# Six gate projections of the merge written behind the convolution's, four kept beside the loads of the first output projection

## The chip, the cores and the metric

The kernel runs on one core of a Trainium2 chip. The metric is the device time of one execution in microseconds (us), as the median of several. The core has five engines with their own instruction rows: TensorE (PE; matmuls, and its weight loads, PEld), VectorE (DVE), ScalarE (ACT), GpSimd (POOL) and SyncE (SP), whose row here only issues DMA transfers. Engines wait for one another by semaphores, and each works off its row in order.

## The reference

One layer of a streaming encoder over 1152 tokens (a prompt of 1024 and eight groups of 16), with a width of 1024. All projections of h share one weight matrix. Branch A is a delta-rule recurrence, branch B a gated short convolution; two gates merge them.

```
h = rmsnorm(x, g_norm)
proj = h @ w_in          # [r k v w a z_a | B C xb z_b | g_a g_b]
...
y, S = wkv7_scan(wkv0, r_h, w_h, kh_h, a_h, v_h, kt_h)
...
out_a = o_a @ w_o_a
gb, gc, xb, z_b = jnp.split(pb, 4, axis=-1)
u = gc * xb
u_pad = jnp.concatenate([conv0, u], axis=1)
cv = sum(conv_w[j] * u_pad[:, j:j + T] for j in range(CONV_W))
out_b = (gb * cv * jax.nn.silu(z_b)) @ w_o_b
g_a, g_b = jnp.split(jax.nn.sigmoid(pg), 2, axis=-1)
x = x + (g_a * out_a + g_b * out_b) @ w_out
x = x + jax.nn.sigmoid(rmsnorm(x, g_ple) @ w_ple_gate) * (p @ w_ple)
```

## The kernel before

Widths of 1024 are eight tiles of 128 partitions, and the 1152 tokens lie along the free axis, in blocks of 512, 512 and 128 (`BLOCKS`, in the order 0, 1024, 512) or three of 384 (`BL3`). A projection tile ("dense") multiplies the eight tiles of h by eight 128x128 weight blocks in a split of two float16 parts: for each block of tokens three matmuls for each of the eight, so 24. `load_w` (L143 to L149) fetches one tile's weights to a stage buffer `wst...` (two of them, SP), makes the high part `whi...` on ACT and the low part `wlo...` on DVE.

The recurrence is cut into 24 steps: eight pairs of heads (7 is the last) by three blocks of tokens (step 7_2 is pair 7, block at 512), 144 chunks of 64 tokens in all. Each chunk is a chain of small matmuls with ACT and DVE work between them (tiles u, vu, sbd, c, xs; the state's copy yst on ACT). What stands ahead of the chain are the prep projections of a step (k, r, v, z), and beside all of it the convolution: `conv(j)` for eight tiles, four projections each (C, x, z_b, B), whose results go to `ob_d` in DRAM. A step's output goes through a normalisation, is turned by a PE transposition (tile py out of yc, L96), gated, and stored to `oa_d` in DRAM.

PE's order of all this is written by hand in `go()`. Seven streams, `chain` to `conv`, are generators; each step of `go()` takes the first stream that is ready by a modelled PE clock, and if none is, a piece of a projection ("fill") from prep or conv:

```
S_chain, S_tail, S_val, S_inv, S_scores, S_prep, S_conv = every = [
    Stream(k) for k in (chain, tail, values, inverse, scores, prep, conv)]
...
fills = more or [x for x in live if x.next == DENSE]
...
pe[0] = min(x.when() for x in live)
```

All other engines, and PE behind `go()`, are ordered by the tile scheduler. It may place PE instructions of the later code between those of the written order where they are free to go.

Behind `go()` comes the merge. `gate(ms[j], T_GB + j)` projects the gate g_b of tile j, with tanh, into the tile ms_j (PE tiles dgb0 to dgb7; weights whigb, wlogb), and `load_o(ob_d, j)` (L919, split at L899 and L901) fetches one tile of branch B's result in three transfers of 384 columns (stage tiles ostb, three buffers) and splits each into ohb (ACT) and olb (DVE). Eight pairs of these stand one behind the other:

```
for j in range(KT):
    gate(ms[j], T_GB + j, f"b{j}")
    obs.append(load_o(ob_d, j, f"b{j}"))
```

Then w_ob is applied: for each j, weights wstb are loaded and split, and three blocks of 24 matmuls (tiles ob) are added up over all eight tiles of obs; DVE (L948) multiplies each with the gate into ms. After it the same for branch A: gates g_a of tiles 0 and 1 (dga), eight loads of `oa_d`, then for each j a block of w_oa (tiles oa), and gate j + 2 behind it. Then w_out (oc), the per-layer embedding and the final norm.

Of the kernel before, what the change touches and what calls it, by code (L numbers as in the profile page):

```python
# [9 lines left out]
F32 = mybir.dt.float32  # L10
# [3 lines left out]
AF = mybir.ActivationFunctionType  # L14
# [6 lines left out]
NTOK = 1152  # L21
BLOCKS = [(0, 512), (1024, 128), (512, 512)]
# [4 lines left out]
IWS = 1.0 / WS  # L27
# [3 lines left out]
T_R, T_K, T_V, T_L, T_ZA, T_B, T_C, T_XB, T_ZB, T_GA, T_GB = 0, 8, 16, 24, 25, 33, 41, 49, 57, 65, 73  # L31
# [35 lines left out]
def build(nc, tc, I, O):  # L67
    with ExitStack() as top:
        _build(nc, tc, I, O, top)


def _build(nc, tc, I, O, top):
    V, A, G, PE, SP = nc.vector, nc.scalar, nc.gpsimd, nc.tensor, nc.sync
# [16 lines left out]
    def mm(out, lhsT, rhs, start, stop):  # L90
        spent(lhsT, rhs, lhsT.dtype == F32)
        PE.matmul(out, lhsT, rhs, start=start, stop=stop)  # L92
# [6 lines left out]
    dram = top.enter_context(tc.tile_pool(name="dram", bufs=1, space=bass.MemoryType.DRAM))  # L99
# [26 lines left out]
    for n, src in enumerate(("w0", "i0", "krep")):  # L126
        o, w = PN[src]
# [14 lines left out]
    def load_w(src, nm):  # L142
        wpool, WR = wcur  # L143
        st = wpool.tile([128, KT, 128], F32, tag="wst", name="wst" + nm, bufs=2)
        SP.dma_start(st, src)
        hi = wpool.tile([128, KT, 128], F16, tag="whi", name="whi" + nm, bufs=WR)
        lo = wpool.tile([128, KT, 128], F16, tag="wlo", name="wlo" + nm, bufs=WR)
        A.activation(hi, st, AF.Copy, scale=WS)  # L148
        V.scalar_tensor_tensor(out=lo, in0=st, scalar=WS, in1=hi, op0=ALU.mult, op1=ALU.subtract)  # L149
        return hi, lo  # L150
# [6 lines left out]
    def hT(k, blk, lo):  # L157
        o, n = blk
        v = hx[:, k, o:o + n].bitcast(F16)
        return v[:, n:2 * n] if lo else v[:, 0:n]  # L160

    def dense_parts(w, blk, nm):

        n = blk[1]
        hi, lo = w
        for k in range(KT):
            yield DENSE if k == 0 else MORE
            if k == 0:
                ps = psd.tile([128, 512], F32, tag="d", name="d" + nm)
            mm(ps[:, :n], hi[:, k, :], hT(k, blk, 0), start=(k == 0), stop=False)  # L170
            mm(ps[:, :n], hi[:, k, :], hT(k, blk, 1), start=False, stop=False)
            mm(ps[:, :n], lo[:, k, :], hT(k, blk, 0), start=False, stop=(k == KT - 1))
        return ps[:, :n]

    def dense(w, blk, nm):
        g = dense_parts(w, blk, nm)
        while True:
            try:
                next(g)
            except StopIteration as e:  # L180
                return e.value
# [4 lines left out]
    for nm_, names, t in (("cpk", CPK, F32), ("cph", CPH, F16)):  # L186
        w = sum(w for _, w in names)
# [17 lines left out]

    oa_d = dram.tile([8, 128, NTOK], F32, tag="oa_d", name="oa_d")
    ob_d = dram.tile([8, 128, NTOK], F32, tag="ob_d", name="ob_d")

    rk = ExitStack()
    wk = rk.enter_context(tc.tile_pool(name="wkv", bufs=2))  # L210
    cvp = rk.enter_context(tc.tile_pool(name="cvp", bufs=1))
# [532 lines left out]
    def conv(j):  # L744
# [43 lines left out]
                                   op0=ALU.mult, op1=ALU.mult)  # L788
        SP.dma_start(ob_d[j], zs)

    pairs = {}
    chunks = [0]
    steps = []
    for j in range(8):
        for g in range(3):
            f = St()
# [22 lines left out]
    class Stream:  # L819
        def __init__(self, kind):  # L820
            self.kind, self.at, self.gen, self.next, self.ready, self.cost = kind, 0, None, None, 0.0, 0.0
            self.till, self.banks = None, 0
            self.total = 8 if kind is conv else len(steps)

        def step(self):
            t = pe[0]
# [21 lines left out]
        def fill(self):  # L848
            return self.next in (DENSE, MORE)

    S_chain, S_tail, S_val, S_inv, S_scores, S_prep, S_conv = every = [
        Stream(k) for k in (chain, tail, values, inverse, scores, prep, conv)]
    may = {S_chain: lambda i: S_inv.at > i and S_val.at > i and S_tail.at >= i - 1,
           S_tail: lambda i: S_chain.at > i,
           S_val: lambda i: S_scores.at > i and S_chain.at >= i - 1 and (i < 2 or steps[i - 2].y_done),
           S_inv: lambda i: S_scores.at > i,
           S_scores: lambda i: S_prep.at > i and (i < 3 or steps[i - 3].y_done),
           S_prep: lambda i: S_chain.at >= i - 3,
           S_conv: lambda i: True}
    CONV_US, LEAD = 8 * 46.4, 4.0  # L860

    def go():
        while True:
            for x in every:
                if x.gen is None and x.at < x.total and may[x](x.at):
                    x.gen = x.kind(x.at if x is S_conv else steps[x.at])
                    x.step()
            live = [x for x in every if x.gen is not None and x.open()]
            if not live:
                return  # L870
            ready = [x for x in live if not x.fill() and x.when() <= pe[0]]
            if ready:
                ready[0].step()
                continue
            more = [x for x in live if x.next == MORE]
            fills = more or [x for x in live if x.next == DENSE]
            if fills:
                behind = S_conv.cost / CONV_US < (chunks[0] + LEAD) / 144
                fills.sort(key=lambda x: (x is S_conv) != behind)
                fills[0].step()  # L880
                continue
            pe[0] = min(x.when() for x in live)

    with tc.manual_schedule(engines={mybir.EngineType.PE}):
        go()
# [10 lines left out]
    ms = [mr.tile([128, NTOK], F32, tag=f"ms{j}", name=f"ms{j}") for j in range(KT)]  # L896

    def split_r(dst_hi, dst_lo, src, scale=1.0):
        A.activation(dst_hi, src, AF.Copy, scale=scale)  # L899
        if scale == 1.0:  # L900
            V.tensor_tensor(out=dst_lo, in0=src, in1=dst_hi.bitcast(F32), op=ALU.subtract)  # L901
        else:
            V.scalar_tensor_tensor(out=dst_lo, in0=src, scalar=scale, in1=dst_hi.bitcast(F32),
                                   op0=ALU.mult, op1=ALU.subtract)

    def load_wr(src, nm, scale=1.0):
        st = ow.tile([128, KT, 128], F32, tag="wst", name="wst" + nm, bufs=2)
        SP.dma_start(st, src)
        wh = op.tile([128, KT, 128], F32R, tag="woh", name="woh" + nm, bufs=2)
        wl_ = op.tile([128, KT, 128], F32R, tag="wol", name="wol" + nm, bufs=2)  # L910
        split_r(wh, wl_, st, scale)
        return wh, wl_

    def load_o(src, k, nm):
        h_ = oo.tile([128, NTOK], F32R, tag=f"oh{k}", name=f"oh{nm}")
        l_ = oo.tile([128, NTOK], F32R, tag=f"ol{k}", name=f"ol{nm}")
        for o, n in BL3:
            st = op.tile([128, 384], F32, tag="ost", name=f"ost{nm}_{o}", bufs=3)
            SP.dma_start(st[:, :n], src[k, :, o:o + n])  # L919
            split_r(h_[:, o:o + n], l_[:, o:o + n], st[:, :n])  # L920
        return h_, l_

    def dense_r(w, src, blk, nm):
        o, n = blk
        wh, wl_ = w
        ps = psp.tile([128, 512], F32, tag="p", name=nm)[:, :n]
        for k in range(KT):
            h_, l_ = src[k]
            mm(ps, wh[:, k, :], h_[:, o:o + n], start=(k == 0), stop=False)
            mm(ps, wh[:, k, :], l_[:, o:o + n], start=False, stop=False)  # L930
            mm(ps, wl_[:, k, :], h_[:, o:o + n], start=False, stop=(k == KT - 1))
        return ps

    def gate(dst, t, nm):
        w = load_w(I["w_in"][t], "g" + nm)
        for o, n in BLOCKS:
            A.activation(dst[:, o:o + n], dense(w, (o, n), f"g{nm}_{o}"), AF.Tanh, scale=0.5 * IWS)

    obs = []
    for j in range(KT):  # L940
        gate(ms[j], T_GB + j, f"b{j}")
        obs.append(load_o(ob_d, j, f"b{j}"))
    for j in range(KT):
        w = load_wr(I["w_ob"][j], f"b{j}")
        for blk in BL3:
            o, n = blk
            ps = dense_r(w, obs, blk, f"ob{j}_{o}")
            V.scalar_tensor_tensor(out=ms[j][:, o:o + n], in0=ms[j][:, o:o + n], scalar=1.0, in1=ps,  # L948
                                   op0=ALU.add, op1=ALU.mult)
    oas = []  # L950
    gts = {}

    def gate_a(j):
        gts[j] = op.tile([128, NTOK], F32, tag="gt", name=f"gt{j}", bufs=2)
        gate(gts[j], T_GA + j, f"a{j}")

    gate_a(0)
    gate_a(1)
    for k in range(KT):
        oas.append(load_o(oa_d, k, f"a{k}"))  # L960
    for j in range(KT):
        w = load_wr(I["w_oa"][j], f"a{j}")
        g = gts[j]
        for blk in BL3:
            o, n = blk
            ps = dense_r(w, oas, blk, f"oa{j}_{o}")
# [28 lines left out]
    xn0 = pgx[:, 2 * KT * D:].rearrange("p (k a t) -> p k a t", a=2, k=KT)  # L995
    gps = small.tile([128, 8], F32, tag="gps", name="gps", bufs=1)
    go, _ = PN["gp"]
    V.tensor_scalar(out=gps, in0=par[:, go:go + 8], scalar1=WS, scalar2=None, op0=ALU.mult)
    xrs, wos = {}, {}
# [186 lines left out]
```

## Time and profile before

| | |
|---|---|
| runs shown | 1945.39, 1945.68 and 3071.51 us, median 1945.68 |
| profiled execution | 1941.51 us, span 1939.7 us |
| busy share of the span | PE 94%, PEld 64%, DVE 65%, ACT 42%, POOL 11% |
| mean clock granted to PE | 0.988 of full speed |
| moved by DMA | 103.57 MB, 53 GB/s on average |

The span is the time between the first and the last instruction of the profiled execution; 1.8 us of it lie outside. The busy share is an average over stages: chunk chain and projections (to about 1195 us), the end of the chain (to about 1335 us), and the merge behind it. Matmuls overlap, so the duration of one is longer than its distance to the next; in PE's rows the starts are compared.

### The profile page before, as it was taken

The numbers are of one execution on the slowest core, as the hardware profiler recorded it, in microseconds if no ns is written. First come the engines' busy times: TensorE is split into PE (matmuls) and PEld (weight loads), VectorE is DVE, ScalarE is ACT, GpSimd is POOL, SyncE is SP. The second block draws the span as 40 slices with busy tenths as digits, with TensorE's granted clock in tenths as the row PEclk, the third lists the DMA queues.
The fourth block names the chain that finished last, engine by engine and source line by source line (L and its number), as shares of the span: only waits on it lengthen the run. The fifth ranks groups of instructions, "written<-read, shape, count | busy, mean of one in ns | idle before, by whom it ended". The sixth has DMA issues, their size and how long they took to land. (4 is left out here: it accounts for less than half of the span.)

```text
span 1939.7 us, 37843 instructions
## 1 busy us (share of the span) xinstructions
PE 1814.9 (94%) x15374; PEld 1248.6 (64%) x15374; DVE 1255.6 (65%) x3225; ACT 811.8 (42%) x1877; POOL 219.1 (11%) x333
## 2 busy tenths in 40 slices
PE   4999999999999999999999998799999999999997
PEld 2565665565566566566556566455698777899766
DVE  7466878787787787787877777774223311444665
ACT  6344545545446446446446445343202211332321
POOL 1010211111111111111111111110000111200000
PEclk9999999999999999999999999899999999999999
DMA  6002011101101101101101100013313311142012
GB/s 217 22 23 76 22 48 42 34 30 60 39 30 50 50 30 50 50 30 37 60 29 37 41 18 15 32 46 94 99 44 96 99 44 33 56 144 87 9 35 78
DMA packets 43758, 103.57 MB, mean 53 GB/s; under 512 B 6208, under 2 KB 21440, under 8 KB 43584
## 3 DMA queue, kind: packets, MB, share of 16 engines
q1 hardware_dynamic: 43584, 101.17, 16.3%
q8 instruction: 120, 1.97, 0.4%
q14 instruction: 54, 0.44, 0.1%
HBM read 84.40 MB, written 16.74 MB: 52 GB/s over the span
## 5 line engine op out<-in xcount | busy, mean ns | idle before, releaser
L92 PEld LDWEIGHTS <-whip 128*128 128x128 f16 x1536 | 132.3, 99 | 72.2 <-issue 3.5
L653 POOL TENSOR_SCALAR Spt<-sbd,pt 128x128 f32<-128x128 f32 x128 | 86.7, 677 | 664.8 <-DVE sbd L669 642.5
L92 PEld LDWEIGHTS <-wlop 128*128 128x128 f16 x768 | 75.4, 98 | 61.1 <-issue 1.1
L669 DVE SCALAR_TENSOR_TENSOR sbd<-u,pt,Spt 64x64 f32<-64x64 f32 x256 | 72.1, 282 | 65.3 <-PE u L92 61.6
L595 ACT ACTIVATE bdgt<-ig 64x512 f16<-64x512 f32 (+1 forms) x208 | 106.5, 512 | 2.5
L659 ACT ACTIVATE yst<-c 64x128 f32<-64x128 f32 x144 | 38.8, 270 | 151.0 <-DVE xs L658 149.7
L92 PE MATMUL dx<-hx,whiX 128*128 128x512 f16 (+1 forms) x384 | 88.4, 326 | 4.7 <-ACT sho L229 4.7
L92 PE MATMUL dgb<-hx,whigb 128*128 128x512 f16 (+1 forms) x384 | 90.5, 331 | 2.2 <-ACT whigb L148 1.6
L92 PE MATMUL dv<-hx,whip 128*128 128x512 f16 (+1 forms) x384 | 90.7, 331 | 0.0
L92 PE MATMUL dzb<-hx,whiZ 128*128 128x512 f16 (+1 forms) x384 | 88.6, 326 | 2.2 <-ACT sho L229 1.8
L92 PE MATMUL dz<-hx,whip 128*128 128x512 f16 (+1 forms) x384 | 89.5, 326 | 0.0
L92 PE MATMUL dC<-hx,whiC 128*128 128x512 f16 (+1 forms) x384 | 88.4, 327 | 1.1 <-ACT cs L750 0.6
L92 PE MATMUL dB<-hx,whiB 128*128 128x512 f16 (+1 forms) x384 | 89.1, 326 | 0.0
L92 PE MATMUL pg<-xn,pg 128*128 128x384 f16 (+1 forms) x576 | 88.9, 309 | 0.0
L92 PE MATMUL dr<-hx,whip 128*128 128x512 f16 (+1 forms) x384 | 88.9, 326 | 0.0
L92 PE MATMUL dk<-hx,whip 128*128 128x512 f16 (+1 forms) x384 | 88.1, 326 | 0.0
L92 PE MATMUL dga<-hx,whiga 128*128 128x512 f16 (+1 forms) x384 | 86.9, 326 | 0.0
L92 PEld LDWEIGHTS <-pg 128*128 128x128 f16 x768 | 66.3, 99 | 27.1 <-issue 2.4
L664 ACT ACTIVATE vu<-u 64x64 f32<-64x64 f32 x288 | 62.3, 216 | 46.8 <-PE u L92 44.1
L589 ACT ACTIVATE gt<-ig 128x512 f16<-128x512 f32 (+1 forms) x104 | 54.3, 522 | 66.0 <-PE ig L92 65.1
L596 DVE CAST_PREDICATED tt<-cph,i 128x512 f16<-128x512 uint16 (+1 forms) x104 | 61.7, 593 | 25.4 <-PE i L92 24.3
L92 PEld LDWEIGHTS u<-xs,tm 128*128 128x128 f32 x288 | 49.7, 192 | 43.9 <-DVE xs L658 28.8
(325 smaller groups left out, 4924.8 us busy)
## 6 DMA issues: line engine op xcount, KB each, us to landing
wstp<-i_w_in SPq DMA_DIRECT2D x32, 512.0 KB, 3.6
xt<-i_x SPq DMA_DIRECT2D x9, 512.0 KB, 5.5
ob_d<-zb SPq DMA_DIRECT2D x8, 576.0 KB, 2.8
ostb<-ob_d SPq DMA_DIRECT2D x24, 192.0 KB, 3.1
osta<-oa_d SPq DMA_DIRECT2D x24, 192.0 KB, 2.9
xr<-i_xT SPq DMA_DIRECT2D x8, 576.0 KB, 3.6
wstC<-i_w_in SPq DMA_DIRECT2D x8, 512.0 KB, 3.5
wstX<-i_w_in SPq DMA_DIRECT2D x8, 512.0 KB, 3.5
```

Of the source, the lines that this page charges most:

```text
L92: PE.matmul(out, lhsT, rhs, start=start, stop=stop)
L589: A.activation(Gt, pg, AF.Copy, scale=-1.0)
L595: A.activation(Gb[R, :, R], pg[R], AF.Copy, scale=-1.0)
L596: V.copy_predicated(out=Tt, mask=bc(lvt[:, b, :]).bitcast(U16), data=p1)
L653: G.tensor_scalar(out=Spt, in0=S, scalar1=pt[:, c:c + 1], scalar2=None, op0=ALU.mult)
L659: A.activation(yst[Vh, p, :], pc[Vh, 0:128], AF.Copy)
L664: A.activation(vu[Uh, c, H], pu[H, H], AF.Copy, scale=-1.0)
L669: V.scalar_tensor_tensor(out=S2[H, H], in0=pu[H, 128 + h * 64:192 + h * 64], scalar=pt[H, c:c + 1], in1=Spt[H, H], op0=ALU.mult, op1=ALU.add)
```

## The change

Gates g_b of tiles 0 to 3 and g_a of tiles 6 and 7 (`EARLY`) are no longer computed in the merge. A new generator, `gates_b`, loads the weights of one of them, runs its three blocks and stores the tanh result to a new DRAM tensor `gb_d`. Its stream, `S_gate`, is the last in the list of `go()` and may run when all eight convolution tiles are through and not all steps are finished, so its projections are fills like theirs. In the merge, ms0 to ms3 and the g_a tiles gt6 and gt7 are read back from `gb_d`. The four g_b gates that are left stand two loads of `ob_d` apart.

```
+    EARLY = [T_GB, T_GB + 1, T_GB + 2, T_GB + 3, T_GA + 6, T_GA + 7]
+    gb_d = dram.tile([len(EARLY), 128, NTOK], F32, tag="gb_d", name="gb_d")
...
+    def gates_b(j):
+
+        w = load_w(I["w_in"][EARLY[j]], f"gb{j}")
+        t = cvp.tile([128, NTOK], F32, tag="cv", name=f"gb{j}", bufs=2)
+        for o, n in BLOCKS:
+            ps = yield from dense_parts(w, (o, n), f"gb{j}_{o}")
+            A.activation(t[:, o:o + n], ps, AF.Tanh, scale=0.5 * IWS)
+        SP.dma_start(gb_d[j], t)
...
-            self.total = 8 if kind is conv else len(steps)
+            self.total = {conv: 8, gates_b: 6}.get(kind, len(steps))
...
-    S_chain, S_tail, S_val, S_inv, S_scores, S_prep, S_conv = every = [
-        Stream(k) for k in (chain, tail, values, inverse, scores, prep, conv)]
+    S_chain, S_tail, S_val, S_inv, S_scores, S_prep, S_conv, S_gate = every = [
+        Stream(k) for k in (chain, tail, values, inverse, scores, prep, conv, gates_b)]
...
-           S_conv: lambda i: True}
+           S_conv: lambda i: True,
+           S_gate: lambda i: S_conv.at == 8 and S_tail.at < len(steps)}
...
-                    x.gen = x.kind(x.at if x is S_conv else steps[x.at])
+                    x.gen = x.kind(x.at if x in (S_conv, S_gate) else steps[x.at])
...
     for j in range(KT):
-        gate(ms[j], T_GB + j, f"b{j}")
-        obs.append(load_o(ob_d, j, f"b{j}"))
+        if T_GB + j not in EARLY:
+            gate(ms[j], T_GB + j, f"b{j}")
+            for k in range(2 * (j - 4), 2 * (j - 3)):
+                obs.append(load_o(ob_d, k, f"b{k}"))
     for j in range(KT):
+        if T_GB + j in EARLY:
+            SP.dma_start(ms[j], gb_d[EARLY.index(T_GB + j)])
         w = load_wr(I["w_ob"][j], f"b{j}")
...
-        gate(gts[j], T_GA + j, f"a{j}")
+        if T_GA + j in EARLY:
+            SP.dma_start(gts[j], gb_d[EARLY.index(T_GA + j)])
+        else:
+            gate(gts[j], T_GA + j, f"a{j}")
```

The order of instructions shows it at three places. The first is PE's row behind the last projection of the convolution, in pair 6's last step. Tiles ig2, i1 and i2 belong to prep of pair 7, u and c to the chain, whig and wlog are the weights of a gate. Before:

```order
L92 MATMUL ig27_0_15901<-tt7_0_15675,bdmh_126 128x64
L92 MATMUL u6_2_3_15862<-vu6_2_15072,kbt6_2_15052 128x128
L92 LDWEIGHTS bdtn_128
L92 MATMUL i127_0_15915<-gt27_0_15910,bdtn_128 128x64
L92 LDWEIGHTS bdtn_128
L92 MATMUL i127_0_15915<-gt27_0_15910,bdtn_128 128x64
...
L92 MATMUL c6_2_4_15927<-sbd0_120,ar6_2_14728 128x128
```

With the change:

```order
L92 MATMUL ig27_0_15909<-tt7_0_15676,bdmh_127 128x64
L92 LDWEIGHTS whigb0_15858
L92 MATMUL dgb0_0_15920<-hx_97,whigb0_15858 128x512
L92 LDWEIGHTS whigb0_15858
L92 MATMUL dgb0_0_15920<-hx_97,whigb0_15858 128x512
L92 LDWEIGHTS wlogb0_15859
L92 MATMUL dgb0_0_15920<-hx_97,wlogb0_15859 128x512
L92 MATMUL u6_2_3_15870<-vu6_2_15073,kbt6_2_15053 128x128
```

Three matmuls of the first early gate stand ahead of the chain's u, and the others follow between its links.

The second place is PE's row around the last transposition, py of step 7_2. The early gates and the late ones have names of the same kind; dgb5 here is a late one, g_b of tile 5. Before:

```order
L92 LDWEIGHTS wlogb3_17561
L92 MATMUL dgb3_0_17564<-hx_97,wlogb3_17561 128x512
L96 MATMUL py7_2_17229<-ident_75,yc7_2_17205 128x128 x4
L92 LDWEIGHTS whigb3_17560
L92 MATMUL dgb3_0_17564<-hx_97,whigb3_17560 128x512
```

With the change:

```order
L92 MATMUL dgb5_1024_17925<-hx_97,whigb5_17895 128x128
L96 MATMUL py7_2_17746<-ident_75,yc7_2_17722 128x128 x4
L92 LDWEIGHTS wlogb5_17896
L92 MATMUL dgb5_1024_17925<-hx_97,wlogb5_17896 128x128
L92 LDWEIGHTS whigb5_17895
L92 MATMUL dgb5_512_17951<-hx_97,whigb5_17895 128x512
```

What stands behind py begins two gates and a block and a half later in the row of gates.

The third is SP's queue at the last store to `oa_d`. Before:

```order
L691 DMA o_wkv_p<-sbd1_121 64x64 x2
L145 DMA wstgb6_17852<-i_w_in 128x1024
L732 DMA oa_d_104<-yc7_2_17205 128x512
L919 DMA ostb0_0_17350<-ob_d_105 128x384
L919 DMA ostb0_384_17354<-ob_d_105 128x384
L919 DMA ostb0_768_17358<-ob_d_105 128x384
L919 DMA ostb1_0_17448<-ob_d_105 128x384
```

With the change:

```order
L960 DMA ms3_17776<-gb_d_106 128x1152
L694 DMA o_wkv_p<-sbd1_122 64x64 x2
L921 DMA wstb0_18230<-i_w_ob 128x1024
L735 DMA oa_d_104<-yc7_2_17722 128x512
L932 DMA ostb0_0_17867<-ob_d_105 128x384
L932 DMA ostb0_384_17871<-ob_d_105 128x384
L932 DMA ostb0_768_17875<-ob_d_105 128x384
L921 DMA wstb1_18315<-i_w_ob 128x1024
L921 DMA wstb2_18400<-i_w_ob 128x1024
L932 DMA ostb1_0_17881<-ob_d_105 128x384
```

The loads of ms and of the first output weight come ahead of the store, and two more weights stand between the first and the second tile of ostb.

## Rows read from the trace of the kernel before

**Rows 1.** Stretch, its length; busy us of PE, PEld, DVE, ACT, POOL; granted clock, DMA.
```profile
75.00:1195.00 1120.00, 1064.61 (x10398) 669.02 (x10396) 870.53 (x2317) 553.83 (x1336) 160.99 (x264) 1.00 0.12 39
1195.00:1335.00 140.00, 118.93 (x1082) 72.56 (x1080) 94.88 (x269) 60.04 (x159) 18.81 (x26) 0.93 0.11 35
1335.00:1400.00 65.00, 63.23 (x390) 36.33 (x391) 20.50 (x32) 22.91 (x44) 0.00 (x0) 1.00 0.41 134
```

**Rows 2.** Timeline of PE: start, duration, operation [idle before, releaser].
```profile
1334.90 0.66 PE L96 MATMUL py<-ident,yc 128*128 128x128 f32 x4 [0.63 <-DVE yc L723]
```

**Rows 3.** Waits of PE, 1195 to 1335: us in total, times, longest.
```profile
PE py L96 <- DVE yc L723: 6.0, 3, 4.8
```

**Rows 4.** Busy time by stretches, columns as in rows 1.
```profile
1224.00:1237.00 13.00, 5.48 (x41) 3.96 (x42) 10.54 (x42) 5.38 (x20) 1.71 (x2) 0.71 0.01 2
1237.00:1255.00 18.00, 15.95 (x112) 9.24 (x110) 10.36 (x25) 4.23 (x14) 1.21 (x2) 0.92 0.05 18
1255.00:1267.00 12.00, 9.41 (x54) 5.02 (x55) 9.36 (x22) 3.97 (x7) 1.28 (x2) 0.57 0.41 140
```

**Rows 5.** Timeline of PE, pairs of projection matmuls at 1238 and 1240.
```profile
1238.27 1.06 PE L92 MATMUL dv<-hx,whip 128*128 128x512 f16 x2
...
1240.56 0.59 PE L92 MATMUL dv<-hx,whip 128*128 128x512 f16 x2
```

**Rows 6.** Timeline of PE, starts of two blocks of a gate.
```profile
1338.68 0.59 PE L92 MATMUL dgb<-hx,whigb 128*128 128x512 f16 x2
...
1343.86 0.59 PE L92 MATMUL dgb<-hx,whigb 128*128 128x512 f16 x2
...
1349.04 0.27 PE L92 MATMUL dgb<-hx,whigb 128*128 128x128 f16 x2
...
1350.38 0.59 PE L92 MATMUL dgb<-hx,whigb 128*128 128x512 f16 x2
```

**Rows 7.** Busy time by stretches, columns as in rows 1.
```profile
1300.00:1326.00 26.00, 24.46 (x155) 13.74 (x156) 10.18 (x37) 8.72 (x29) 5.18 (x7) 1.00 0.09 26
400.00:500.00 100.00, 91.57 (x891) 59.01 (x890) 79.67 (x226) 47.23 (x122) 10.96 (x23) 1.00 0.15 48
100.00:200.00 100.00, 96.69 (x903) 57.94 (x901) 70.42 (x175) 48.77 (x112) 12.58 (x19) 1.00 0.16 51
```

**Rows 8.** Costliest groups: weight loads of prep, busy us, mean ns.
```profile
L92 PEld LDWEIGHTS <-whip 128*128 128x128 f16 x1536 | 132.3, 99 | 72.2 <-issue 3.5
```

**Rows 9.** Timeline of PE, in the first block of ob, 22 matmuls apart.
```profile
1393.34 0.33 PE L92 MATMUL ob<-ohb,wolb 128*128 128x384 f32 x1
...
1397.17 0.33 PE L92 MATMUL ob<-ohb,wohb 128*128 128x384 f32 x1
```

**Rows 10.** Timeline of ACT: a gate's weights, two triples of ob_d.
```profile
1343.84 1.06 ACT L148 ACTIVATE whigb<-wstgb 128x1024 f16<-128x1024 f32 x1 [0.31 <-PE dgb L92]
...
1351.09 1.02 ACT L899 ACTIVATE ohb<-ostb 128x384 fp32r<-128x384 f32 x2 [1.25 <-DMA ostb<-ob_d]
...
1358.10 1.03 ACT L899 ACTIVATE ohb<-ostb 128x384 fp32r<-128x384 f32 x2
```

**Rows 11.** Timeline of DVE: a gate's weights, the last triple, the first result.
```profile
1371.94 1.23 DVE L149 SCALAR_TENSOR_TENSOR wlogb<-wstgb,whigb 128x1024 f16<-128x1024 f32 x1
...
1375.19 1.15 DVE L901 TENSOR_TENSOR olb<-ostb,ohb 128x384 fp32r<-128x384 f32 x2 [2.02 <-ACT ohb L899]
...
1397.37 0.56 DVE L948 SCALAR_TENSOR_TENSOR ms<-ms,ob 128x384 f32<-128x384 f32 x1 [20.14 <-PE ob L92]
```

**Rows 12.** DMA issues: operation, count, KB each, median us to landing.
```profile
ostb<-ob_d SPq DMA_DIRECT2D x24, 192.0 KB, 3.1
...
wstgb<-i_w_in SPq DMA_DIRECT2D x8, 512.0 KB, 3.6
```

**Rows 13.** Busy time of DVE and ACT on the tile yst, two stretches.
```profile
1195.00:1335.00 140.00, 2.34 (x4) 5.93 (x22) 0.93 0.11 35
480.00:800.00 320.00, 3.31 (x6) 10.28 (x38) 1.00 0.13 43
```

## The prediction

> **What bounds the kernel now.** I read the shares of the engines first, by stretches of the span [rows 1]. From 75 to 1195 us, while projections are still left for the written order to fill with, TensorE (PE) is busy for 1064.61 of 1120 us. From 1195 to 1335 us, when the last convolution projection is through and only the chunk chain is left, it is busy for 118.93 of 140 us, at a granted clock of 0.93. Behind that, through the gates and loads, it is at 63.23 of 65 us. So the kernel is bound by PE throughout, with one hole of 21.1 us between the end of the convolution and the last transposition of the chain (py of step 7_2), which starts at 1334.90 and takes 0.66 us [rows 2]. The waits of PE in the hole say that it stands for links of the chain, above all for VectorE's yc, 6.0 us in three waits with one of 4.8 [rows 3]: latency that other matmuls could cover.
>
> The clock makes the hole larger. Before 1237 us PE is at work for 5.48 of 13 us, and behind this its granted clock lies between its levels of 1.2 and 2.4 GHz, at 0.71, 0.92 and 0.57 of full speed in three stretches [rows 4]. Two matmuls of 512 columns take 1.06 us at 1238.27 and 0.59 two microseconds later [rows 5]. A clock of 0.71 over 13 us means 7.5 us at the lower level; times the busy share of 0.42, and half of that as excess, 1.6 us. The other two stretches give 18 x 0.16 x 0.89 / 2 = 1.3 and 12 x 0.86 x 0.78 / 2 = 4.0. Together 6.9 us of the 118.93 are slow clock, not work: the hole holds 112.0 us of work at full speed in 140 us.
>
> **What the change moves.** One gate is 24 matmuls for each of its blocks of 512, 512 and 128 columns: 5.18 us (1338.68 to 1343.86) twice, and 1.34 us (1349.04 to 1350.38), 11.70 us in all [rows 6]. I counted the gate matmuls in PE's row before and after the change. Ahead of the last py stand 159 of 512 columns and 72 of 128 before, which the scheduler had put there from gb0 to gb3; with the change 360 and 191 stand there: the six early gates, all of gb4 and most of gb5. The first of them stands right behind the last convolution projection and takes turns with the chain. So 201 x 0.2158 = 43.4 us and 119 x 0.056 = 6.6 us, together 50.0 us, move ahead of the last py. No matmul is added or taken away; what can be won is time in the hole, what can be lost is cover behind it.
>
> **The hole (gain R).** The stretch from 1195 us to the last py then holds 112.0 + 50.0 = 162.0 us of work. How dense will it be? The nearest row is the end of the hole, where the chain already had scheduler-placed gates beside it: 24.46 busy of 26 us, 94.1%, at a clock of 1.00 [rows 7]. At that share it takes 172.2 us, so py starts at about 1367.2. The old hole and the moved work one after the other would be 140 + 50 = 190, so R = 17.8 us. The bounds come from the loaded stage: its loosest and its densest stretch of 100 us are busy for 91.57 and 96.69 us [rows 7], which give 176.9 and 167.5 us, R from 13.1 to 22.5.
>
> Busy time of matmuls overlaps, so it may flatter. The Trainium skill (Perfetto Trace Analysis, Identifying the Most-Contended Engine) says that matmul busy time is a bad measure and that the weight loads' busy share should be used. By that row, the loaded stage shows 669.02 of 1120 us, 59.7%, and the hole 72.56 of 140, 51.8%; 320 added loads of 0.099 us [rows 8] make 104.2, at 59.7% that is 174.5 us, and R would be 15.5, the sum 2.3 us lower. The order of the two stretches is the same by both measures.
>
> **The loads of the first output projection (loss S).** Eight triples of ost loads must be split by ScalarE (ohb) and VectorE (olb) before the first block ob0_0 can end. They still begin after the last py in both kernels, since their pool takes memory that the last store of the chain (oa_d of 7_2) frees. Before, 4.72 gates lay over them, 55.3 us; now one matmul of gb5's 128 block, gb5's last block, gb6 and gb7: 28.6 us of PE work. ob0_0 itself is 24 x 0.174 = 4.2 us (22 matmuls from 1393.34 to 1397.17) [rows 9], so without a stall it would end 33.5 us after py starts (0.66 + 28.6 + 4.2). When is the last triple there? Triples follow each other on ScalarE at 3.5 us when nothing else holds them up: two of them from 1351.09 to 1358.10 [rows 10]. By the order of SP's queue a load of the second output weight stands ahead of the second triple and waits, by way of VectorE, for gb7's weights to be split, which need gb5's last block to be done: 5.2 us after py, plus 1.06 on ScalarE and 1.23 on VectorE [rows 10, 11], so about 7.6. A load lands in 3.1 us [rows 12]; then seven triples at 3.5 end near 34 to 35 us after py, a stall of about 2 us. If they keep the pace of before, where the last split needed is through 40.8 us after py (the two pieces from 1375.19, 1.15 us long, against the end of py at 1335.56) [rows 2, 11], the stall is 7.6 us. Before's pace includes the gaps of gate evictions and weight loads on SP, of which half are gone; I take 4.5. PE's clock has dropped after such a gap in the hole, so I add 1 us, between 0 and the 4.0 us of the worst of the three stretches above. Against that, PE's own idle time of 65 - 63.23 = 1.8 us there [rows 1] goes. S = 4.5 + 1 - 1.8 = 3.7 us net, with 0.2 and 9.8 as ends.
>
> **What costs nothing.** The six early gates write 576 KB each to DRAM and are read back into ms0 to ms3 and gt6, gt7. A load of 512 KB lands in 3.6 us [rows 12], one of 576 KB in about 4; ms0 to ms3 are asked for before the last oa_d store and needed 33 us later, and gt6 and gt7 are read while one output-projection step of some 12.5 us (72 x 0.174) runs. Uncovered, both gt loads would be 8 us. ga6 and ga7 leave the stage of the second output projection: 23.4 us of PE work at full clock there, the same at the front. Their weight loads go along; six more splits of 1.06 us (ScalarE) and 1.23 us (VectorE) in the hole, where ScalarE is busy for 60.04 and VectorE for 94.88 of 140 us [rows 1]; the early gates' evictions go to ScalarE as before.
>
> **The sum.** 17.8 - 3.7 = 14.1 us. On the profiled execution's 1941.51 us that is 1927.4; this execution lies 4.2 us below the median of 1945.68, which makes **1932** for the median (1931.6).
>
> **The rivals.**
> (a) Late loads. The splits keep before's pace and PE comes back from the stall at half clock: S = 7.6 + 4.0 - 1.8 = 9.8, gain 8.0, 1937.7. For it: PE's longest wait in the hole, 4.8 us [rows 3], lies just ahead of the pair that takes 1.06 us [rows 5]. Against it: fewer ScalarE jobs between the splits. The Trainium skill (TensorE: Matmul & The Clock Gate, HAM oscillation) tells of a kernel in which every wait for data was followed by matmuls at half clock; by that rule the drop follows any long stall, the 1 us in the sum would be 4, and the forecast 1934.6; the trace agrees for that one wait.
> (b) The chain sets the hole, not the share. In the loaded stage 38 chunks (by the yst copies, 38 on ScalarE) take 320 us, 8.42 us a chunk [rows 13]; 22 chunks are left after 1195 us (the same count on ScalarE in the hole). If the early gates slow the chain to that pace it takes 185.3 us, R = 4.7, gain 1.0, 1944.7. For it: the fill rule takes a gate step whenever the modelled clock sees the chain wait. Against it: in the loaded stage there is more fill for a chunk (prep and convolution) than here.
> (c) Slower. The new stream loads its gate's weights in its own first line, where prep and convolution have theirs asked for ahead. If each early gate stood for its weights, it would be the load's 3.6 us [rows 12] and the two splits, 5.9 us, six times: 35 us, 1945.7 - 14.1 + 35 = 1966.6. It decides from 14.1 / 6 = 2.35 us uncovered per gate. Against it: in SP's queue these loads stand one gate ahead or more, with two stage buffers, and the splits have no wait on a late matmul.
> (d) Denser than taken: R = 22.5 and S = 0.2, gain 22.3, 1923.4.
> That the change does not do what it says is excluded by the rows of the order.
>
> **Chances and range.** Forecast, with its own range of 1928 to 1936: 0.53. (a) 0.15, (b) 0.13, (c) 0.07, (d) 0.12. The range goes from 1923 (d) to 1946 (b, with the bound that nothing is won), which leaves (c) and the outer parts. About 2% is what a measurement of this kernel can tell from no change, 38.9 us: faster than 1906.8 needs more than the whole hole of 21.1 + 6.9 us, slower than 1984.6 more than (c). So 0.01, 0.98, 0.01.
>
> **What the changed profile would show.** Clock 1.00 and about 94% busy from 1195 to 1367 us, with the last py at 1367 (1362 to 1372); if it is at 1380, (b) holds. Between py and the first ob block a wait of PE for olb of 2 to 8 us; without one, S is too large. The first result of the first block at about 1406, where it was at 1397.37 [rows 11]. Waits of PE for whigb or wlogb of over 2 us at the starts of six gates would mean (c). From there to the end 23.4 us less than before. The prediction is wrong if py comes later than 1372 or the stall is over 8 us, or if the stage of oa, with two gates less, opens a wait of its own for gt6, gt7 or weights.

## The result and the profile after

The changed kernel took 1916.69 us as the median of four runs (1915.24 to 1923.96), against 1945.54 before: a ratio of 0.9861, with a 95% interval of 0.9832 to 0.989. Ratios here and below are of the fast executions alone; one of before's four took 3071.51 us. Timed once more beside other kernels it came to 0.9876 (0.9859 to 0.9892). By the ratios the gain is 24 to 27 us, where 14 were forecast, and the time lies below the lower end of the range, 1923. The profiled execution took 1915.24 us, its span 1913.5.

The busy time of the engines by stretches, after. The first row answers to the second of [rows 1]: from the convolution's end to the last py, by the start of each one's last matmul.

```profile
1190.50:1355.90 165.40, 160.36 (x1446) 99.08 (x1445) 100.44 (x277) 70.67 (x179) 17.42 (x26) 0.99 0.20 72
1195.00:1250.00 55.00, 54.27 (x493) 34.53 (x491) 43.62 (x124) 28.78 (x76) 7.35 (x12) 1.00 0.13 44
1250.00:1290.00 40.00, 37.62 (x381) 24.27 (x380) 22.55 (x54) 17.84 (x42) 4.79 (x6) 0.96 0.24 87
1290.00:1355.90 65.90, 64.09 (x516) 36.97 (x515) 30.11 (x91) 20.12 (x53) 5.28 (x8) 1.00 0.22 81
1355.90:1390.00 34.10, 31.28 (x176) 15.67 (x175) 15.37 (x25) 15.94 (x31) 0.00 (x0) 0.95 0.56 176
```

PE is now busy for 160.36 of the 165.4 us, 97%, at a clock of 0.99. Before, the same stretch (by its own trace from 1192.6 to 1335.3) was 142.7 us long with 121.63 busy at 0.93. So 50.0 us of gates were put in and the stretch grew by 22.7: R = 27.3 us. The last row is the place behind py: 2.8 us idle and a clock of 0.95, where [rows 1] has 1.8 us of idle time and 1.00.

The waits of PE, first from the convolution's end to py, then from py to 1400 us (total, times, longest). They answer to [rows 3].

```profile
PE c L92 <- DVE sbd L672: 2.5, 2, 2.3
PE py L96 <- DVE yc L726: 0.9, 1, 0.9
PE u L92 <- DVE xs L661: 0.5, 1, 0.5
PE i L92 <- ACT bdgt L598: 0.2, 1, 0.2
...
PE dgb L92 <- ACT ms L950: 2.8, 2, 2.3
```

Of the 6.0 us for yc 0.9 are left. No wait for whigb or wlogb is in the list, so rival (c) did not happen. The last py starts at 1355.9, before the 1362 to 1372 that the prediction named. The wait behind py is not the expected one for olb: PE waits for the eviction of a gate's block (ms).

VectorE's first result of the first output block, which answers to the last of [rows 11]:

```profile
1394.20 0.55 DVE L965 SCALAR_TENSOR_TENSOR ms<-ms,ob 128x384 f32<-128x384 f32 x1
```

The timeline of PE at py, which answers to [rows 2], and at the two waits behind it:

```profile
1355.50 0.66 PE L96 MATMUL py<-ident,yc 128*128 128x128 f32 x4 [0.92 <-DVE yc L726]
...
1368.40 0.59 PE L92 MATMUL dgb<-hx,whigb 128*128 128x512 f16 x2 [0.49 <-ACT ms L950]
...
1382.60 0.59 PE L92 MATMUL dgb<-hx,whigb 128*128 128x512 f16 x2 [2.34 <-ACT ms L950]
```

From the last of py's four matmuls to the first result it was 62.1 us before (1335.3 to 1397.37) and is 38.3 now (1355.9 to 1394.20); from the first result to the end of the span 542.3 and 519.3, 23.0 less for the 23.4 us of ga6 and ga7. With the convolution ending 2.1 us earlier, which is chance (below), the four pieces are +22.7 - 23.8 - 23.0 - 2.1 = -26.2, the difference of the spans.

### The profile page after: what moved, and what is told of

Its sections match the earlier page's. It is cut to its first block, busy times and chain, and to the rows that moved or that the text cites. A ratio compares the mean times of both kernels' runs of the same rounds, so it can differ in the third digit from the quotient of the medians.

```text
span 1913.5 us, 37852 instructions
## 1 busy us (share of the span) xinstructions
PE 1805.2 (94%) x15374; PEld 1247.2 (65%) x15374; DVE 1254.9 (66%) x3225; ACT 814.1 (43%) x1877; POOL 218.3 (11%) x333
## 4 chain that ended last, share of the span: by engine, by line
PE 66%; DVE 21%; ACT 6%; issue 3%; DMA 2%; POOLq 0%; POOL 0%; SPq 0%; DVEq 0%; ACTq 0%
PE ob L92 5%; PE oc L92 5%; PE oa L92 5%; PE dk L92 4%; PE dr L92 4%; PE dgb L92 4%; PE pg L92 4%; PE dz L92 4%; PE dga L92 4%; PE dC L92 3%; PE dx L92 3%; PE u L92 3%; PE dzb L92 2%; PE dv L92 2%; PE i L92 1%
## 5 line engine op out<-in xcount | busy, mean ns | idle before, releaser
L92 PE MATMUL dgb<-hx,whigb 128*128 128x512 f16 (+1 forms) x480 | 114.0, 332 | 2.8 <-ACT ms L950 2.8
L92 PE MATMUL dgb<-hx,wlogb 128*128 128x512 f16 (+1 forms) x240 | 76.2, 331 | 0.0
```

## The experiments

Single executions of one kernel reach the end of the convolution at different times (1190.5 and 1195.8 us in the two traces of the changed kernel), though PE's order up to there is the same before and after. Behind this point the stretch to py repeats to 0.1 us in these two traces (165.4 both times), py to the first result to 0.9 us, and the whole way to the end to 1.7 us. So besides the ratios I use three lengths from each trace: the hole (start of the convolution's last matmul to the start of py's last), py to the first result, and from the hole's start to the end of the span. A difference of under 2 us in the last of them is not told from chance. Gate work put in is counted in PE's order against the kernel before, with the 0.2158 and 0.056 us of the prediction.

```
kernel            put in   hole   PE busy  busy less put in   py to result   hole to end
before               0     142.7   121.63       121.6             62.1          747.1
extra2_again       21.2    144.3   134.53       113.3             68.1          754.1
extra4             36.0    153.6   147.32       111.3             73.2          768.2
early4             36.0    153.6   147.31       111.3             37.1          730.8
changed            50.0    165.4   160.36       110.4             38.3          723.0
changed, again     50.0    165.4   160.43       110.4             39.2          721.3
early8             65.9    177.2   172.69       106.8             46.4          718.6
early10_ost6       78.7    190.3   185.76       107.1             57.5          720.0
ost6               50.0    164.1   158.99       109.0             38.8          719.6
dve_split          50.0    165.6   160.38       110.4             39.2          724.1
dve_split_ost6     50.0    163.9   158.96       109.0             33.2          715.7
early8_ost6        65.9    177.2   172.71       106.8             44.3          717.4
early8_dve_ost6    65.9    177.3   172.69       106.8             41.9          715.0
```

The five holes with 50.0 us put in differ by the clock: it was 0.99 in the changed kernel, in its repetition and in dve_split, and 1.00 in the two runs with six buffers, whose hole is about 1.4 us shorter. PE's order in it is the same.

**Work that nothing needs, put in the hole.** The merge as before, and the new stream with gates whose results nobody reads (the merge computes all sixteen again). Against the changed kernel:

```
-    EARLY = [T_GB, T_GB + 1, T_GB + 2, T_GB + 3, T_GA + 6, T_GA + 7]
+    EARLY = [T_GB, T_GB + 1]                    # extra4: T_GB to T_GB + 3
...
-            self.total = {conv: 8, gates_b: 6}.get(kind, len(steps))
+            self.total = {conv: 8, gates_b: len(EARLY)}.get(kind, len(steps))
...
+        gate(ms[j], T_GB + j, f"b{j}")
+        obs.append(load_o(ob_d, j, f"b{j}"))
...
```

> The kernel before, with two gate projections more in the written order behind the convolution's (loaded, computed, stored, read by nobody; the merge computes all sixteen gates itself): 23.4 us of PE work that nothing needs. Theory A (the hole of before is nearly all free room: 21.1 us idle, and 11 us of its busy time are slow clock and unoverlapped latency of lone matmuls): the last py stays within 3 us of 1335 us or comes earlier, the time within 3 us of before. Theory B (the prediction's sizes: 112.0 us of work at 94.1%): the last py about 2 us later, the time about 4 us over before. Rival C (the gain of the change is in the merge, the hole has little room): the time 15 us or more over before.

> As the run with two, with four gate projections more that nothing reads: 46.8 us of added work. By the order 36.0 us more of projection work stand ahead of the last py and 10.8 us of the merge's own gates move behind it. A: the stretch from the convolution's end to py is (108.7 + 36.0) / 0.97 = 149 us against 142, plus 10.8 behind: 18 us over before. B: (114 + 36.0) / 0.941 = 159, plus 10.8: 28 us over before. C: 47 us over before.

> Two gate projections more that nothing reads, once more, since the profile of the first run fell in an execution with a lower clock throughout. From the convolution's end to py 142.6 us in the kernel before, 153.5 with 36.0 us more put in, here 21.2 more: if the room is a mere sum of idle time, slow clock and latency, 140 to 143 us and the time within 3 us of before; if each us put in costs 0.3 from the start, 149 us, and 6 to 9 us over before (2.1 us of the merge's gates move behind py).

Measured: two gates 1.0032 of before (1.0015 to 1.0049), in the repetition 1.0033 (1.0018 to 1.0048), 6 to 7 us; four gates 1.0102 (1.0073 to 1.013), 20 us. Of the two runs with two gates the repetition's trace is read. In the hole 21.2 us of work cost 1.6 us, and 36.0 cost 10.9. With two gates the rest lies behind py (68.1 us against 62.1): 2.1 us of gate work moved there, and PE's waits and a fall of its clock (0.97 over this stretch, where it was 1.00) make up the others. So 23.4 us of unneeded work cost 6 to 7 us and 46.8 cost 20: the room is there, and it is not the merge that gives the gain (C falls). Two gates do not tell A from B: the hole grew by 1.6 us (within A's 3 us, and near B's 2), the time by more than either said, since what happened behind py was in neither theory. Four gates put the hole, at 153.6 us, between A's 149 and B's 159, and the time (20 us over before) nearer to A's 18 than to B's 28. So the room is larger than the prediction's sizes and smaller than A's. Nor does every us put in cost 0.3 from the start, as the repetition's second theory had it (149 us): the hole took 144.3.

**Four early gates.** `EARLY` with the four g_b alone, ga6 and ga7 back in the merge.

> The changed kernel with only the four g_b gates early; ga6 and ga7 go back into the merge. By the order 74.3 us of gate work stand ahead of py (88.3 with six) and only 23.4 us behind it. A (hole full either way, ga6 and ga7 pay by leaving gb4 and gb5 as cover over the loads): py about 12 us earlier than with six, a stall of 8 to 10 us in front of the first output block, time 1918 to 1924. Rival (gain grows with the number of gates put in the hole): py's stretch as dense as with six, no more stall, time about 1916 plus the two gates' share of a third of the 27 us, 1925 or more. Rival (the two g_a gates are neutral): 1916.

Measured: 0.9906 (0.9877 to 0.9935), 1923.48 us. By the ratios that is 6 to 9 us slower than the changed kernel, with intervals that just overlap; from the hole's start to the end it is 730.8 us against 723.0 and 721.3. The hole is 153.6 us, exactly that of extra4, whose order ahead of py is the same, and 11.8 shorter than with six, as A expected. Behind py stand only 19.3 us of gates, and PE waits there for the splits (its waits from 1352 to 1392 us):

```profile
PE ob L92 <- ACT ohb L912: 4.1, 4, 2.1
PE dgb L92 <- ACT ms L950: 0.7, 1, 0.7
```

With the first block (4.2 us), 21 matmuls of the second that the scheduler put between (3.7 us), and py's own end, 27.5 us of work stand before the first result; it takes 37.1. That is a stall of 9.6 us, within the 8 to 10 that A expected: 5.1 us of waits, and behind them slow clock (0.57 from 1378 to 1382 us and again from 1388 to 1392). The two g_a gates are thus not neutral: they hand over gb4 and most of gb5 as work that fits in the hole (2.3 us of R) and as cover over the loads (some 4 us).

**Eight early gates.**

> The changed kernel with ga4 and ga5 early too, eight gates in the written order. By the order 104.2 us of gate work stand ahead of py and 40 us behind it. A (the hole is full at 97%, what is put in more moves py by as much, but the loads behind py are covered again): py near 1371, stall in front of the first output block gone (2.8 us of idle time and the slow clock after it), time 1910 to 1914. Rival (fills beyond six get in the chain's way, each link waits behind a block): py later than 1378, time 1918 or more.

Measured: 0.9869 (0.9847 to 0.9891), not told from the changed kernel's 0.9861 and 0.9876. The hole is 177.2 us: 15.9 more us put in cost 11.8, so it was not full at six, where A had it full (some 1.4 of the 4.1 us saved are the clock, 1.00 here), and the fills are not in the chain's way (the rival had py later than 1378; it starts at 1372.7). But the stall is still there, though 36.2 us of gates stand behind py: PE waits 3.5 us for ms, in its list from 1372 to 1420 us. More cover does not end it; A is wrong there, and its 1910 to 1914 us are missed (1918.17).

```profile
PE dgb L92 <- ACT ms L950: 3.5, 2, 1.7
```

**Where the stall behind py comes from.** In the trace of the changed kernel ScalarE's row has, before PE's wait of 2.34 us ends at 1382.60:

```profile
1381.00 1.06 ACT L912 ACTIVATE ohb<-ostb 128x384 fp32r<-128x384 f32 x2 [1.38 <-DMA ostb<-ob_d]
1381.97 0.58 ACT L950 ACTIVATE ms<-dgb 128x512 f32<-128x512 f32 x1
```

The eviction of a gate's block stands behind splits, and these wait for a load. The kernel gives such blocks two buffers (pool `psd`), and PE stands still until one is evicted. First I took the stage buffers for the cause:

```
-            st = op.tile([128, 384], F32, tag="ost", name=f"ost{nm}_{o}", bufs=3)
+            st = op.tile([128, 384], F32, tag="ost", name=f"ost{nm}_{o}", bufs=6)
...
```

The tag's three later uses change in the same way.

> The changed kernel with six stage buffers for the loads of the output projections (and for the three later uses of the same tag) in place of three. Theory D (the stall behind py comes from gate evictions that stand on ScalarE behind splits, and these wait for stage buffers): the two waits of PE for ms behind py, 2.8 us, go, with the slow clock after them; py to first result falls from 38.7 to 34 or 35 us; 3 to 4 us faster than the changed kernel, ratio to before 0.983 to 0.985. Rival (the loads themselves are the limit, by their 3.1 us each or the weights between them in SP's queue): py to first result 37 us or more, ratio 0.986.

> Eight early gates (ga4 and ga5 with them) and six stage buffers. D: stall behind py gone, py to first result from 46.4 to 42 us; with the hole as in the run with eight gates (177 us from the convolution's end to py), the stretch from the convolution's end to the program's end 713 to 715 us against 722.6 with the change, ratio to before 0.981 to 0.983. Rival (loads limit): as the run with eight, 718 us, 0.987.

> Ten early gates (g_b 0 to 3, g_a 2 to 7) and six stage buffers. By the order 117.0 us of gate work stand ahead of py, 78.7 more than before, and four whole gates behind it. If room is left in the hole (each us moved there moved py by 0.30 us up to 36, 0.84 from 36 to 50, 0.74 from 50 to 66): 177 + 12.8 x 0.8 = 187 us to py, and 2 to 3 us faster than with eight, ratio 0.980 to 0.982. If it is full at eight: 190 us or more, the same time as with eight.

Measured: 0.9866 (0.9848 to 0.9884) with six gates, 0.9846 (0.9824 to 0.9869) with eight, 0.987 (0.9855 to 0.9884) with ten. With six gates py to the first result stays at 38.8 us: the loads are done some 10 us earlier, and still one eviction stands behind one split that waits for its load. ScalarE's row in this run:

```profile
1381.23 0.52 ACT L912 ACTIVATE ohb<-ostb 128x384 fp32r<-128x384 f32 x1 [2.01 <-DMA ostb<-ob_d]
1381.66 0.58 ACT L950 ACTIVATE ms<-dgb 128x512 f32<-128x512 f32 x1
```

PE's wait for it is longer than in the changed kernel:

```profile
PE dgb L92 <- ACT ms L950: 3.8, 1, 3.8
```

So the buffers alone do not end the stall, and D is wrong there; its other half, evictions behind splits in ScalarE's row, is seen again in these rows. With eight gates the six buffers take 2.1 us off the way from py to the first result (46.4 to 44.3), half of what D expected. Ten gates: the hole takes 190.3 us, 13.1 more for 12.8 put in, at a clock of 0.99 against 1.00, so the room ends at about eight.

Then I took the splits out of ScalarE's row (the buffers left at three, then six, then with eight gates):

```
-            split_r(h_[:, o:o + n], l_[:, o:o + n], st[:, :n])
+            if src is ob_d:
+                V.tensor_copy(h_[:, o:o + n], st[:, :n])
+                V.tensor_tensor(out=l_[:, o:o + n], in0=st[:, :n], in1=h_[:, o:o + n].bitcast(F32), op=ALU.subtract)
+            else:
+                split_r(h_[:, o:o + n], l_[:, o:o + n], st[:, :n])
```

> The changed kernel once more, beside the next three on the same chip: ratio to before 0.986 as in its first timing, and a second trace of it, for how far the end of the convolution and the stretches behind it vary between executions of one kernel (theory: several us at the end of the convolution, under 1 us in the stretches counted from there).

> The changed kernel with the high part of the ob_d tiles made by VectorE in place of ScalarE, so that no split that waits for a load stands ahead of a gate eviction in ScalarE's row. Theory E (the stall behind py is the order in ScalarE's row, not the stage buffers and not the loads): the waits of PE for ms behind py, 2.8 us, fall under 1 us, py to first result from 38.7 to 34 or 35 us unless the loads end too late for the first block; 2 to 4 us faster than the changed kernel. Rival (the loads' pace is next): PE waits for olb instead, as long, and nothing is won.

> As the run with VectorE's splits, with six stage buffers. E with the loads' pace as the next limit: no wait of PE for ms or olb behind py over 1 us, py to first result 34 to 35 us, 4 us faster than the changed kernel, ratio 0.984. If the loads are no limit: the same as the run with VectorE's splits alone.

> Eight early gates, VectorE's splits and six stage buffers: the candidate for the fastest. 4 us for the stall and 0 to 4 for the two further gates: ratio to before 0.981 to 0.985, below the changed kernel's on the same chip.

Measured on one chip: the changed kernel 0.9876 (0.9859 to 0.9892), VectorE's splits alone 0.9884 (0.9869 to 0.9899), with six buffers 0.9836 (0.9816 to 0.9857), with eight gates as well 0.9835 (0.982 to 0.9849). The waits of PE from py on, with VectorE's splits alone:

```profile
PE ob L92 <- DVE ohb L934: 2.2, 1, 2.2
PE dgb L92 <- ACT ms L954: 1.6, 1, 1.6
PE py L96 <- DVE yc L726: 0.9, 1, 0.9
```

With six buffers too the list has one line, the wait ahead of py:

```profile
PE py L96 <- DVE yc L726: 0.9, 1, 0.9
```

Alone, neither edit wins anything that the ratios show. With the splits gone from ScalarE, PE waits 2.2 us for the splits themselves, which the three buffers make late (the rival of E). The 1.6 us for ms are ScalarE's row once more: the evictions now stand behind the split of an output weight, which has stayed there and waits for its own load. ScalarE's row in this run:

```profile
1372.47 1.06 ACT L912 ACTIVATE wohb<-wstb 128x1024 fp32r<-128x1024 f32 x1 [4.40 <-DMA wstb<-i_w_ob]
1373.44 0.74 ACT L954 ACTIVATE ms<-dgb 128x512 f32<-128x512 f32 x2
```

The first of the changed kernel's two waits, 0.49 us, has the same cause. With both edits the stall is gone, and PE is busy for the whole stretch from py to the first result, at full clock (columns as in [rows 1]):

```profile
1355.20:1388.40 33.20, 33.20 (x198) 19.14 (x197) 23.55 (x54) 6.66 (x11) 0.00 (x0) 1.00 0.72 234
```

The same stretch in the run with six buffers alone:

```profile
1354.70:1393.60 38.90, 35.12 (x198) 19.59 (x197) 17.34 (x30) 17.57 (x35) 0.00 (x0) 0.96 0.61 200
```

198 matmuls in 33.2 us or in 38.9: the stall costs 5.7 us, 3.8 of waiting and 1.9 more of busy time, with the clock at 0.66 just behind the wait:

```profile
1384.00:1388.00 4.00, 4.00 (x14) 1.51 (x13) 0.18 (x1) 0.00 (x0) 0.00 (x0) 0.66 0.52 163
```

The two kernels with both edits, at 1910.38 and 1910.8 us, beat the changed one (1919.31 beside them) by 0.4%; from the hole's start to the end they take 715.7 and 715.0 us against 721.3. Of the 9 us between the medians the stall makes 5 to 6, and some 1.4 are the clock in the hole. Two further gates add nothing that can be measured.

## Why the prediction was wrong

The direction, the place and the mechanism were right: the gain comes from the hole between the convolution's end and py, part of it is given back behind py, and the moved g_a gates leave the later stage without a new wait there. The size was wrong, and **the step that failed is the term R of the hole**: 17.8 us, with a bound of 22.5, where 27.3 were measured. Both of its factors were off: of the 9.5 us that it lacked, 5.2 are idle time (16.1 us of it went, 10.9 had been taken) and 4.3 are busy time (11.2 and 6.9).

- **The density.** I took 94.1% from 26 us of the old trace in which the chain had scheduler-placed gates beside it. With gates between all links the stretch is 97% busy: 5.0 us stay idle, not 10.2. The row was a thin one, and it ended a little above the upper bound (96.69% from the loaded stage).
- **The work.** I counted all busy time that was not slow clock as work: 112.0 us from 1195, 114.7 from the convolution's end (121.6 less 6.9). The busy time of the old work falls as more is put beside it: 121.6, 113.3, 111.3, 110.4, 106.8 us in the table, at clocks of 0.93, then 0.99 to 1.00; with six gates and a clock of 1.00 it is 109.0. So some 6 us at six gates (and 8 at eight) were neither work nor slow clock. The mean durations of PE's groups do not show where. Two of the chain's, in the whole hole before, in its first part before (1195 to 1224 us, clock 1.00), and in the whole hole after:

```profile
L92 PE MATMUL u<-vu,kbt 128*128 128x128 f32 x42 | 10.4, 331 | 3.3 <-ACT vu L664 2.3
L92 PE MATMUL psc<-ar,kb 64*64 64x128 f32 x80 | 3.9, 303 | 0.5 <-DVE scy L493 0.5
...
L92 PE MATMUL u<-vu,kbt 128*128 128x128 f32 x10 | 2.2, 301 | 0.2 <-ACT vu L664 0.2
L92 PE MATMUL psc<-ar,kb 64*64 64x128 f32 x16 | 0.8, 280 | 0.0
...
L92 PE MATMUL u<-vu,kbt 128*128 128x128 f32 x42 | 9.1, 298 | 0.7
L92 PE MATMUL psc<-ar,kb 64*64 64x128 f32 x80 | 2.9, 277 | 0.0
```

  The means fell from 331 to 298 ns and from 303 to 277, but at full clock they were 301 and 280 before, so most of this is slow clock. What shrank is the time that a matmul holds PE until the next one starts. Counted so in the traces (to the next start, or to its own end where that comes first), the 893 matmuls of the hole that belong to no gate cover 76.6 us before and 67.3 after; away from the slow clock it is 0.080 and 0.075 us for one, some 5 us for all. A lone matmul is shown busy until its modelled end; with another right behind it the two overlap. That this is all of the 6 us is not shown.

The measure of the weight loads, which the prediction set beside this, gave R = 15.5 and was further off: their share came out as it took it (95.78 us of the 160.9 from 1195 to py, 59.5%, where 59.7% had been taken), but the loads' busy time grew by 23.2 us, not by the 31.7 that 0.099 us each make.

**The loss S** was 3.7 us net. Measured: py to the first result is 33.2 us without a stall (dve_split_ost6) and 38.3 and 39.2 in the two traces, so a stall of 5.1 to 6.0 where 5.5 had been taken (4.5 and 1), less before's own idle time. Counted by the order, 26.7 us of gates left this stretch (55.3 to 28.6) and it got 23.8 shorter, 22.9 in the second trace: 2.9 to 3.8 us net. The size was right by luck, for its place and its cause were wrong: I had PE waiting for olb in front of the first block, and it waits inside the late gates, for evictions queued on ScalarE behind splits that wait for loads. I had named that stage's loads and not who shares their engine's row. That PE's clock drops after such a wait (0.91 from 1370 to 1390) was expected, at 1 us; in ost6 the busy time beyond work was 1.9, so neither that nor the 4 of rival (a).

The row that I set for (a) was misread. Before's clock had fallen ahead of its wait of 4.84 us, which begins at 1231.2, and stayed low through it; that wait did not bring it down:

```profile
1228.00:1230.00 2.00, 0.79 (x6) 0.58 (x6) 1.77 (x9) 1.17 (x6) 0.00 (x0) 0.87 0.00 0
1230.00:1232.00 2.00, 0.91 (x5) 0.68 (x4) 1.29 (x9) 0.97 (x5) 0.00 (x0) 0.50 0.00 0
...
1236.08 1.11 PE L96 MATMUL py<-ident,yc 128*128 128x128 f32 x4 [4.84 <-DVE yc L723]
```

**What was taken at nothing** stayed so: the stores to gb_d land in 2.9 us, the gt tiles in 3.7, the ms tiles in 6.7 (about 4 had been taken), and PE waits for none of them. Behind the first result the stage with two gates less took 23.0 us less in the first trace and 25.7 in the second, for 23.4 us of gates. Of the rivals, (a) is half true (the slow clock behind the stall), (b) and (c) are not (the chain is not slower, no gate waits for its weights), and (d), the denser hole, is the one that came, beyond its own bound. About 2 us of the first trace are chance: the convolution ended 2.1 us earlier than in the trace of before, but 3.2 later in the second trace of the same kernel.

## What to carry to other kernels

The room in a stretch that is bound by latency is more than its idle time: to it come the slow clock, and the part of the busy time that lone matmuls show because nothing follows them. Put some work that nobody reads into it and see what it costs; here 21 us cost 1.6, 36 cost 10.9, and the step from 66 to 79 us cost its own length. When cover is moved away from a stage of loads, look at the row of the engine that splits them: whatever else it serves, such as evictions, waits for those loads in order; here neither more buffers nor another engine for the splits helped alone.

## What the runs showed of the hardware that was not expected

The same order of instructions up to the end of the convolution reached it between 1190.5 and 1198.7 us in the thirteen traces used here. In the four of them whose granted clock never falls between 60 us and there it came at 1190.5 to 1192.5; in the three with three falls at 1194.9 to 1198.7. Before's trace shows one such loss from 1090 to 1100 us, where the granted clock was 0.83 and the changed kernel's was 1.00, with the same wait of PE just ahead of it (2.04 us for bdtn in both). Why the clock falls in one execution and not in the next stays open. Two waits of PE of 1.7 us each in the run with eight gates were followed by no drop (1.00 from 1390 to 1430), one of 2.34 us in the changed kernel by 0.91 (1370 to 1390).
